# Low halves of the weights made a whole load at a time, over the load itself, and eight load buffers in turn

## The chip, the cores and the metric

One core of one Trainium2 chip runs the kernel. The metric is device time in microseconds for one execution, and a lower number is better. Three runs of the kernel before gave 504.73 to 505.06, median 504.81.

## The reference

The input `x` has 512 rows of 1,024 floats. It is normalised by row, multiplied with `w_in` (1,024 x 6,936) and cut into the inputs of two mixers that work side by side:

```python
h = rms_norm(x, norm_pre)
proj = h @ w_in
(q_n, k_c, v_c, k_s, v_s, k_w, v_w, g_n, z_n,
 q_r, k_r, v_r, z_r, m_a, m_b) = jnp.split(proj, split_points(), axis=-1)
...
y_a = (o_a * jax.nn.silu(z_n)) @ w_nsa_o
...
q_r = apply_rotary(q_r.reshape(B, S, RET_HEADS, RET_QK_DIM), ret_ang)
k_r = apply_rotary(k_r.reshape(B, S, RET_HEADS, RET_QK_DIM), ret_ang) * (RET_QK_DIM ** -0.5)
o_b = jax.vmap(retention_sequence)(q_r, k_r, v_r.reshape(B, S, RET_HEADS, RET_V_DIM))
y_b = (o_b * jax.nn.silu(z_r)) @ w_ret_o
merged = jax.nn.sigmoid(m_a) * y_a + jax.nn.sigmoid(m_b) * y_b
x = x + rms_norm(merged @ w_out, norm_post)
```

`o_a` is sparse attention with a compressed, a selected and a sliding branch (8 heads of 64, two key groups; the compressed keys and values come from a small network with the weights `cmp_w1`, 2,048 x 256, and `cmp_w2`). `o_b` is retention in chunks of 128 rows (4 heads). `apply_rotary` turns pairs of columns that lie half a head apart; the retention heads have 128 columns, all of them turned.

## The kernel before

**Splitting.** A float32 weight is used as the sum of two fp32r numbers, a high half (the rounded weight) and a low half (what rounding left), and so is the other operand. Each product is made of three matmuls: high by high, high by low, low by high (`mm3`). TensorE's work is these matmuls and the transposes (line 263).

**The stream.** All weights lie in one array in the order of use, cut into loads of 128 partitions by 1,024 columns (512 KB; four loads have 560). SyncE's queue issues them (`load_next`, lines 427 and 430) into four buffers `raw`. A load is two *pieces* of 512 columns. For each piece `splitter` has ScalarE (sometimes VectorE, `cp_any`) copy the piece to `whi` (lines 224 and 232), and `split_lo` has VectorE subtract, `wlo = raw - whi` (line 236). `whi` and `wlo` are rings of `NW` = 9 tiles of 512 columns. A piece holds its two tiles until the last matmul that reads it (`used_up`); a buffer `raw` is loaded again as soon as the low halves of both its pieces are made. Some loads (tables of sums for Strassen-like products, the 280-column block, the last four loads) are split into places of their own instead of the ring.

**Stages.** `main` runs them in order: the first block (8 pieces, each used for all four row tiles before the next), a 280-column block, the queries (8 pieces, used once for each of the four row tiles), `hidden` (16 pieces for `cmp_w1`, each used once by four matmuls of 256 columns, while attention's scores, transposes and products stand between them), then the blocks of `PLAN` (gates, retention's inputs, output projections) and `out_seven`. An ordinary block's piece is read in four passes, one for each row tile. Retention's rotation is `tail_qk`: four products of 256 columns with the row's scale and a table (line 249), then a subtraction and an addition. `vals` writes the attention's values as high and low halves, two copies and two subtractions of 64 columns.

**Order.** The program is recorded by a planner (`Order`): coroutines give the time at which they could go on, by a cost for each instruction; the planner takes the first by priority that is due within a margin of its own (`MARGINS`, by coroutine). The order on each engine's queue is fixed by that. `SOON`, `PSOON`, `SLACK` and the hold times belong to the same rules. `load_next` is recorded when a buffer is planned to be free, so the loads stand in SyncE's queue among its other transfers (rotation tables, line 1100, and the signed rows of `x` for the sums, line 606). GpSimd's queue adds up weight sums in DRAM meanwhile (lines 395 and 397).

## Time and profile before

| what | value |
|---|---|
| median of three runs | 504.81 us |
| profiled execution | 504.99 us |
| its span, first to last instruction | 503.2 us |
| TensorE busy | 493.7 us (98%) |
| VectorE busy | 424.6 us (84%) |
| ScalarE busy | 324.7 us (65%) |
| granted TensorE clock, mean | 0.998 |
| instructions | 7,872 |

A busy span of TensorE is not TensorE at its peak, since matmuls overlap: what a matmul costs is read from the distance between the starts of two neighbours. In the same way two VectorE instructions of one kind in a row take less than twice one of them. The chain of waits follows the execution back from its end, and each wait names the last releaser.

### The profile page before, as it was taken

Reading aid. Unit: us, or ns where it says so; the run is one execution under the profiler, and the core shown is the slowest. Engines: PE = TensorE matmul, PEld = TensorE weight load, DVE = VectorE, ACT = ScalarE, POOL = GpSimd, SP = SyncE. Lnnn points to the kernel's source line nnn. Section 1 sums busy time; section 2 is a strip of 40 time slices with the busy share of each in tenths; the row PEclk is TensorE's granted clock in tenths of the full one; section 3 lists DMA queues with packets and bytes.
Section 4 is the critical chain, followed back from the end, with each engine's and each line's share of the span. In section 5 each row is a group of like instructions: output and inputs, shape, how many; then the busy total and the mean of one; then the engine's idle time right before and its main releaser. Section 6 shows DMA issues by size and latency. Waiting matters only on the chain.

```text
span 503.2 us, 7872 instructions
## 1 busy us (share of the span) xinstructions
PE 493.7 (98%) x2666; PEld 421.4 (84%) x2666; DVE 424.6 (84%) x996; ACT 324.7 (65%) x722; POOL 39.3 (8%) x66
## 2 busy tenths in 40 slices
PE   8999999999999999999999999999999999999994
PEld 7898887888888888888888888888888989988883
DVE  6698899989989989998789999778787867979795
ACT  6795599558679788784587574835435535527642
POOL 3102100023000210000100000101000000000010
PEclk9999999999999999999999999999999999999999
DMA  8968995779998899325556673530473735635813
GB/s 318 385 211 283 326 227 200 242 136 225 370 238 182 262 293 211 113 85 166 119 173 212 215 235 114 126 126 8 162 250 113 233 116 191 199 113 169 303 56 142
DMA packets 31080, 98.75 MB, mean 196 GB/s; under 512 B 3136, under 2 KB 6976, under 8 KB 30272
## 3 DMA queue, kind: packets, MB, share of 16 engines
q1 hardware_dynamic: 24576, 70.85, 41.5%
q0 software_dynamic: 6320, 27.26, 22.9%
q8 instruction: 21, 0.34, 0.3%
q14 instruction: 19, 0.16, 0.1%
q10 hardware_dynamic: 144, 0.14, 0.1%
HBM read 93.52 MB, written 31.98 MB: 249 GB/s over the span
## 4 chain that ended last, share of the span: by engine, by line
PE 89%; DMA 5%; DVE 4%; issue 1%; ACT 0%; POOLq 0%; DVEq 0%; POOL 0%; ACTq 0%; SPq 0%
PE bank L257 70%; PE bank L1234 8%; PE bank L1725 7%; PE bank L263 4%; DMA raw<-in_stream_dram 3%; DVE arena_r L236 1%; DMA words<-in_xT_dram 1%; DVE wlo L236 1%; DMA words<-in_x_dram 1%; DVE words L236 1%; DVE words L679 0%; DVE words L249 0%; DVE words L243 0%; DVE words L967 0%; DVE whi L232 0%
## 5 line engine op out<-in xcount | busy, mean ns | idle before, releaser
L224 ACT ACTIVATE whi<-raw 128x512 fp32r<-128x512 f32 x177 | 107.0, 627 | 53.4 <-PE bank L257 36.2
L236 DVE TENSOR_TENSOR wlo<-raw,whi 128x512 fp32r<-128x512 f32 x188 | 123.4, 685 | 10.4 <-ACT whi L224 9.5
L257 PE MATMUL bank<-whi,hTh 128*128 128x512 f32 x192 | 74.0, 407 | 0.3 <-ACT hTh L224 0.3
L257 PE MATMUL bank<-arena_r 128*128 128x256 f32 (+2 forms) x328 | 70.7, 335 | 0.7 <-DVE arena_r L236 0.5
L257 PE MATMUL bank<-whi,hTl 128*128 128x512 f32 x192 | 71.2, 391 | 0.0
L257 PE MATMUL bank<-wlo,hTh 128*128 128x512 f32 x192 | 71.0, 390 | 0.0
L224 ACT ACTIVATE arena_r<-bank 128x512 fp32r<-128x512 f32 (+3 forms) x104 | 49.1, 476 | 26.3 <-PE bank L263 25.4
L236 DVE TENSOR_TENSOR arena_r<-bank,arena_r 128x512 fp32r<-128x512 f32 (+3 forms) x104 | 56.0, 542 | 9.6 <-ACT arena_r L224 8.5
L257 PE MATMUL bank<-arena_r,whi 128*128 128x512 f32 (+1 forms) x208 | 63.6, 381 | 0.0
L224 ACT ACTIVATE words<-words,stat 128x128 f32<-128x128 f32 (+3 forms) x105 | 54.1, 546 | 6.6 <-DVE stat L967 4.9
L257 PEld LDWEIGHTS bank<-arena_r 128*128 128x128 f32 x328 | 50.8, 189 | 7.6 <-DVE arena_r L236 1.2
L257 PE MATMUL bank<-hTh,whi 128*128 128x512 f32 (+1 forms) x144 | 52.2, 363 | 0.0
L257 PE MATMUL bank<-hTh,wlo 128*128 128x512 f32 (+1 forms) x144 | 51.4, 357 | 0.0
L257 PE MATMUL bank<-hTl,whi 128*128 128x512 f32 (+1 forms) x144 | 51.1, 355 | 0.0
L257 PEld LDWEIGHTS bank<-arena_r,whi 128*128 128x128 f32 x208 | 38.8, 188 | 7.3
L257 PEld LDWEIGHTS bank<-whi,hTl 128*128 128x128 f32 x192 | 36.2, 188 | 8.0
L257 PEld LDWEIGHTS bank<-whi,hTh 128*128 128x128 f32 x192 | 36.5, 191 | 6.9 <-ACT hTh L224 0.6
L257 PEld LDWEIGHTS bank<-wlo,hTh 128*128 128x128 f32 x192 | 36.1, 188 | 6.3
L257 PE MATMUL bank<-arena_r,wlo 128*128 128x512 f32 x96 | 37.3, 389 | 0.0
L263 PEld LDWEIGHTS bank<-identr,shorts 128*128 128x128 f32 x268 | 30.1, 140 | 8.6 <-DVE arena_r L236 0.9
L224 ACT ACTIVATE words<-words 128x512 f32<-128x512 f32 (+3 forms) x47 | 27.2, 586 | 12.8 <-DVE words L236 8.0
L263 PE MATMUL bank<-identr,shorts 128*128 128x128 f32 x268 | 31.6, 238 | 0.5 <-DVE arena_r L236 0.5
(182 smaller groups left out, 891.0 us busy)
## 6 DMA issues: line engine op xcount, KB each, us to landing
raw<-in_stream_dram SPq DMA_DIRECT2D x73, 512.0 KB, 4.4
pair<-in_stream_dram POOLq DMA_DIRECT2D x6, 1024.0 KB, 11.8
t<-in_stream_dram POOLq DMA_DIRECT2D x6, 1024.0 KB, 17.2
out<-in_stream_dram POOLq DMA_DIRECT2D x6, 1024.0 KB, 17.1
words<-in_x_dram SPq DMA_DIRECT2D x8, 512.0 KB, 6.9
raw<-s SPq DMA_DIRECT2D x8, 512.0 KB, 4.2
raw<-pair SPq DMA_DIRECT2D x8, 512.0 KB, 4.2
raw<-t SPq DMA_DIRECT2D x8, 512.0 KB, 3.6
```

Of the source, the lines that this page charges most:

```text
L224: S.activation(o, i, func, **kw)
L236: (V if e == "dve" else G).tensor_tensor(o, a, b, op=op)
L257: T.matmul(ps, a, b, start=start, stop=stop)
L263: T.transpose(ps, a, idn)
L1234: T.matmul(ps[m], a, b, start=n in first and s + j == 0, stop=n in last and s + j == 5, skip_group_check=True)
L1725: T.matmul(ps[m], a, b, start=n in first and s + i == 0, stop=n in last and s + i == 5, skip_group_check=True)
```

## The change

The low half of a whole load is made in one subtraction of 1,024 columns and written over the load: each of `NR` = 8 buffers has two names, `raw` (float32) and `rest` (fp32r), at the same address. The tiles `wlo` are gone; `whi` is a ring of five tiles of 1,024 columns (`NW` = 10 pieces), still copied 512 columns at a time. A buffer whose low half lies in it is vacant only when both its pieces are used up; a load that is split into a place of its own frees its buffer after the split. The buffers are taken in the order in which they become vacant. Retention's query and key columns are permuted in the stream, so that the two columns of a rotated pair are neighbours, and `tail_qk` makes two products of 512 columns in place of four of 256. `vals` makes one copy and one subtraction of 2 x 64 columns. One small addition in `ret` goes from VectorE to GpSimd. The planner's table and a score of priorities are other numbers.

```diff
-NR, NW = 4, 9
+NR, NW = 8, 10
...
-MARGIN = 50.0
+MARGIN = 600.0
...
-SOON = 2
-PSOON = 4
+SOON = 4
+PSOON = 3
...
-    nc.alloc_sbuf_tensor("room", [P, 58 * 256], FT)
-    low, made = nc.sbuf_base - 58 * 1024, {}
+    nc.alloc_sbuf_tensor("room", [P, 58 * 256 + NR * 1024 + 128], FT)
+    low, made = nc.sbuf_base - 58 * 1024 - NR * 4096 - 512, {}
+    rawt = [[nc.alloc_sbuf_tensor_at(f"{n}{i}", [P, 1024], dt, offset=low + 58 * 1024 + 320 + i * 4096)
+             for n, dt in (("raw", FT), ("rest", FR))] for i in range(NR)]
...
+    vacant, room = [(0.0, i) for i in range(NR)], []
+
+    def own(i):
+        return KD <= 2 * i < 2 * KD or i in sload or i >= len(loads) - 4
+
+    def may_load():
+        return len(raws) < len(loads) and bool(vacant)
...
-            raw = rp.tile([P, 1024], FT, name="raw", tag="raw", bufs=NR)
-            o, c, r = loads[i][0], 0, parts[2 * (i - NR) + 1][2] if i >= NR else 0.0
...
+        r, b = vacant.pop(0)
+        room.append(b)
+        raw = rawt[b][0].ap()
...
         done.append(r)
+        i = len(done) // 2 - 1
+        if len(done) % 2 == 0 and not own(i):
+            vacant.append((r, room[i]))
+        while may_load():
+            load_next()
...
-                    hi = wp.tile([P, 512], FR, name="whi", tag="whi", bufs=NW)
-                    lo = wp.tile([P, 512], FR, name="wlo", tag="wlo", bufs=NW)
...
+                        hi, lo = wp.tile([P, 1024], FR, name="whi", tag="whi", bufs=NW // 2), rawt[room[i]][1].ap()
...
-                od.spawn(split_lo(p, hi, lo, src, vh, vl, e), rank(p))
+                es.append(e)
                 nxt[0] = p + 1
+                if k:
+                    od.spawn(split_lo(i, hi, lo, src, max(es)), rank(2 * i))
...
-            r = sub_split(vl, src, vh, r)
-        yield lambda: len(parts) == p
-        parts.append((hi, lo, r))
-        if p % 2 and len(raws) <= p // 2 + NR:
-            load_next()
+            r = sub_split(lo[:, :n], src, hi[:, :n], r)
+        yield lambda: len(parts) == 2 * i
+        for k in range(2):
+            c = slice(k * n // 2, (k + 1) * n // 2)
+            parts.append((hi[:, c], lo[:, c], r))
+        if own(i):
+            vacant.append((r, room[i]))
+            while may_load():
+                load_next()
...
-        for g in range(2):
-            sv = src[:, g * 64:(g + 1) * 64]
-            e = act(VS[:, t, br, g, g, :], sv, r=r)
-            e = sub_split(VS[:, t, br, g, 1 - g, :], sv, VS[:, t, br, g, g, :], e)
-        return e
+        sv, b = src.rearrange("p (g c) -> p g c", g=2), VS[:, t, br, 0, 0, :]
+        hi, lo = (bass.AP(tensor=b.tensor, offset=b.offset + o, ap=[list(b.ap[0]), [n, 2], [1, 64]]) for o, n in ((0, 192), (64, 64)))
+        return sub_split(lo, sv, hi, act(hi, sv, r=r))
...
-                    od.spawn(att_unit(t, g, brs, slots, stat), 2)
+                    od.spawn(att_unit(t, g, brs, slots, stat), 0)
...
-        for i in range(2):
-            e = stt(v1[:, :, i, :], pv[:, :, i, :], rs(t), tv[:, 0], OP.mult, OP.mult, e)
+        c = [tv[:, i].unsqueeze(2).broadcast_to([P, 256, 2]) for i in range(2)]
+        e = stt(v1, pv, rs(t), c[0], OP.mult, OP.mult, e)
         yield e, "dve"
-        stt(v2[:, :, 0, :], pv[:, :, 1, :], rs(t), tv[:, 1], OP.mult, OP.mult, e)
-        e = stt(v2[:, :, 1, :], pv[:, :, 0, :], rs(t), tv[:, 1], OP.mult, OP.mult, e)
+        e = stt(v2, pv, rs(t), c[1], OP.mult, OP.mult, e)
...
-        ev = ts(rv, mv[:, :, 1], 1e-6, None, OP.add, r=e)
+        G.tensor_scalar(rv, mv[:, :, 1], 1e-6, None, op0=OP.add)
+        ev = od.op("pool", 80.0, e, True)
```

Three places show how the order moved. The first is VectorE's queue at the very start, where `raw_55` (before: `raw`) is the first load and `hTl` the low half of the normalised input's first 128 columns. Before:

```order
L483 CAST whi<-raw 128x512
L249 SCALAR_TENSOR_TENSOR hTl<-words_264_165,hTh 128x256
L249 SCALAR_TENSOR_TENSOR hTl<-words_512_108,words_264_165,hTh 128x256
L243 TENSOR_SCALAR ngp<-words_264_165 128x8
L236 TENSOR_TENSOR wlo<-raw,whi 128x512 x2
```

After:

```order
L498 CAST whi<-raw_55 128x512
L237 TENSOR_TENSOR rest_56<-raw_55,whi 128x1024
L250 SCALAR_TENSOR_TENSOR hTl<-words_264_178,hTh 128x256
L250 SCALAR_TENSOR_TENSOR hTl<-words_512_121,words_264_178,hTh 128x256
L244 TENSOR_SCALAR ngp<-words_264_178 128x8
L233 CAST whi<-raw_57 128x512
```

The weights' low half, which needs both high halves, stands ahead of the input's low half, where it stood behind it.

The second is VectorE's queue in the middle of `hidden`, where `arena_r<-bank` is the low half of transposed attention weights, `stat` a softmax sum and `ISA` the largest score of a row. Before:

```order
L236 TENSOR_TENSOR arena_r<-bank_88,arena_r 128x512
L232 CAST whi<-raw 128x512
L236 TENSOR_TENSOR wlo<-raw,whi 128x512 x3
L236 TENSOR_TENSOR arena_r<-bank_89,arena_r 128x512
L253 RECIPROCAL stat_857<-stat_857 128x4
L236 TENSOR_TENSOR stat_857<-stat_857,gate 128x4
L236 TENSOR_TENSOR wlo<-raw,whi 128x512
L236 TENSOR_TENSOR arena_r<-bank_88,arena_r 128x512
```

After:

```order
L233 CAST whi<-raw_61 128x512
L233 CAST whi<-raw_55 128x512
L237 TENSOR_TENSOR rest_62<-raw_61,whi 128x1024
L237 TENSOR_TENSOR rest_56<-raw_55,whi 128x1024
L237 TENSOR_TENSOR words_128_709<-words_512_141,cst 128x128
L237 TENSOR_TENSOR words_128_710<-words_512_141,cst 128x8x8 x2
L237 TENSOR_TENSOR words_512_141<-words_128_709,words_128_710 128x8x16
L254 RECIPROCAL stat_814<-stat_814 128x4
L237 TENSOR_TENSOR stat_814<-stat_814,gate 128x4
L237 TENSOR_TENSOR arena_r<-bank_101,arena_r 128x512
L237 TENSOR_TENSOR arena_r<-bank_102,arena_r 128x512
L237 TENSOR_TENSOR rest_58<-raw_57,whi 128x1024
```

Low halves of `hidden` now stand ahead of the attention's work instead of among it, and a cast of the load `raw_55`, the first of `hidden`'s second half, stands ahead of the low halves `rest_62` and `rest_56`.

The third is SyncE's queue after the signed rows, from the load that follows the first rotation table. Before, by the numbers of the buffers' uses:

```order
L606 DMA s0_148<-words14336_512_115 128x256
L606 DMA s2_150<-words14336_512_115 128x256
L1100 DMA words28672_512_136<-in_rope_r_dram 128x512
L427 DMA raw_906<-in_stream_dram 128x1024
L427 DMA raw_954<-in_stream_dram 128x1024
```

After:

```order
L628 DMA s2_163<-words14336_512_128 128x256
L1120 DMA words28672_512_149<-in_rope_r_dram 128x512
L437 DMA raw0_55<-in_stream_dram 128x1024
L437 DMA raw1_57<-in_stream_dram 128x1024
L437 DMA raw4_63<-in_stream_dram 128x1024
L437 DMA raw5_65<-in_stream_dram 128x1024
L437 DMA raw2_59<-in_stream_dram 128x1024
```

All loads of `hidden`'s first half stand ahead of this table in the queue in both kernels. `raw0_55` is its fifth load, the first of its second half; in the changed kernel it waits until TensorE has read the first load of the queries for the last time, where before it waited for low halves to be made.

## The prediction, made before the changed kernel was run

> **What bounds the kernel now.** I read the page first, then busy time by stretches, then TensorE's timeline where a stretch is not full.

> ```profile
> span 503.2 us, 7872 instructions
> PE 493.7 (98%) x2666; PEld 421.4 (84%) x2666; DVE 424.6 (84%) x996; ACT 324.7 (65%) x722; POOL 39.3 (8%) x66
> PE 89%; DMA 5%; DVE 4%; issue 1%; ACT 0%; POOLq 0%; DVEq 0%; POOL 0%; ACTq 0%; SPq 0%
> ```

> The chain of waits is TensorE for 89%. So the floor is TensorE's own work, and only time in which it waits can be won. Its pace where nothing disturbs it (columns: start, length, instruction), and its end:

> ```profile
> 485.63 5.60 PE L1725 MATMUL bank<-arena_r 128*128 128x512 f32 x24
> ...
> 496.29 0.39 PE L1725 MATMUL bank<-arena_r,hTh 128*128 128x512 f32 x1
> ```

> 24 matmuls take 5.60, of which the last one has 0.39 for itself: 5.21 for 23 steps, 0.227 us for 512 columns. After the last one (496.29 + 0.39) come 6.5 us of norm and output.

> Busy time by stretch (length, then PE, PEld, DVE, ACT) shows where TensorE isn't full:

> ```profile
> 71.00:85.00 14.00, 12.58 (x86) 10.47 (x85) 13.58 (x33) 13.91 (x31) 0.00 (x0) 1.00 0.70 221
> ```

> From 71 to 85 us, in `hidden`, VectorE and ScalarE are both over 96% busy and TensorE is not. A piece of `hidden` costs TensorE only four matmuls of 256 columns, the splitting engines as much as any other. The waits there, in TensorE's timeline:

> ```profile
> 73.03 0.45 PE L257 MATMUL bank<-arena_r 128*128 128x512 f32 x1
> 74.02 0.50 PE L257 MATMUL bank<-arena_r 128*128 128x512 f32 x1 [0.54 <-DVE arena_r L236]
> ...
> 75.30 0.28 PE L257 MATMUL bank<-wlo,arena_r 128*128 128x256 f32 x1
> 75.42 0.28 PE L257 MATMUL bank<-whi,arena_r 128*128 128x256 f32 x1
> 76.16 0.38 PE L257 MATMUL bank<-wlo,arena_r 128*128 128x256 f32 x1 [0.47 <-DVE wlo L236]
> ...
> 82.29 0.28 PE L257 MATMUL bank<-wlo,arena_r 128*128 128x256 f32 x1
> 82.87 0.54 PE L263 MATMUL bank<-identr,shorts 128*128 128x128 f32 x4 [0.30 <-DVE arena_r L236]
> ```

> The first step is 0.99 us where 0.23 would do, the second (75.42 to 76.16) 0.74 for the 0.12 of a normal one (75.30 to 75.42), the third 0.58 for 0.12: 0.76 + 0.62 + 0.46 = 1.84 us. Smaller steps of the same kind up to 86 us (for instance 83.94 to 84.33) bring it to about 3.0 by my count of starts, so 1.2 of it is an estimate from many rows.

> **The start: slower by 0.74.** TensorE, VectorE and ScalarE in the first microseconds:

> ```profile
> 4.71 2.02 PE L257 MATMUL bank<-whi,hTh 128*128 128x512 f32 x4 [0.30 <-ACT hTh L224]
> 6.56 1.07 PE L257 MATMUL bank<-whi,hTl 128*128 128x512 f32 x4
> ...
> 4.69 0.48 DVE L249 SCALAR_TENSOR_TENSOR hTl<-words,hTh 128x256 fp32r<-128x256 f32 x1 [0.38 <-ACT hTh L224]
> 5.09 0.48 DVE L249 SCALAR_TENSOR_TENSOR hTl<-words,words,hTh 128x256 fp32r<-128x256 f32 x1
> ...
> 4.96 0.61 ACT L224 ACTIVATE whi<-raw 128x512 fp32r<-128x512 f32 x1
> ```

> Today `hTl` is ready at 5.17, long before TensorE asks for it at 6.56. In the new order the low half of the first load stands ahead of it on VectorE, and that one needs ScalarE's second high half, ready at 4.96 + 0.61 = 5.57. Its length is that of the only subtraction of 1,024 columns in the trace:

> ```profile
> L236 DVE TENSOR_TENSOR arena_r<-words,arena_r 128x1024 fp32r<-128x1024 f32 x2 | 2.4, 1213 | 0.0
> L236 DVE TENSOR_TENSOR wlo<-raw,whi 128x512 fp32r<-128x512 f32 x188 | 123.4, 685 | 10.4 <-ACT whi L224 9.5 <-PE bank L257 0.4
> ```

> 5.62 + 1.21 = 6.83, less 0.07 of overlap and plus 0.48 gives 7.24, and 0.06 later TensorE goes on: 7.30 for 6.56. The second half of `hTl`, 0.40 later, is in time for the third matmul (7.30 + 0.45). Bounds: 0.4 if the subtraction starts earlier, 1.1 if its full length is kept. Later low halves of the first block are ready a microsecond or more ahead, and so hide.

> **`hidden`: faster by 1.8.** Prices on VectorE are distances between starts; the first row is TensorE's first score in the old order:

> ```profile
> 59.87 0.63 PE L257 MATMUL bank<-arena_r 128*128 128x512 f32 x2
> ...
> 58.56 0.55 DVE L236 TENSOR_TENSOR words<-words,cst 128x128 f32<-128x128 f32 x3
> ...
> 60.53 0.69 DVE L967 CUSTOM_DVE_ANT_0 words<-bank,maskp 128x512 f32<-128x512 f32 x1 [0.97 <-PE bank L257]
> ...
> 62.09 1.39 DVE L236 TENSOR_TENSOR arena_r<-bank,arena_r 64x512 fp32r<-64x512 f32 x2
> ...
> 65.55 0.69 DVE L236 TENSOR_TENSOR wlo<-raw,whi 128x512 fp32r<-128x512 f32 x1
> 66.16 0.68 DVE L967 CUSTOM_DVE_ANT_0 words<-bank,maskp 128x512 f32<-128x512 f32 x1
> 66.77 0.08 DVE L967 DVE_READ_ACCUMULATOR2_ANT stat<- 128x1 f32 x1
> ...
> 73.89 0.42 DVE L232 CAST whi<-raw 128x512 fp32r<-128x512 f32 x1
> 74.22 1.89 DVE L236 TENSOR_TENSOR wlo<-raw,whi 128x512 fp32r<-128x512 f32 x3
> ...
> 84.19 1.89 DVE L236 TENSOR_TENSOR wlo<-raw,whi 128x512 fp32r<-128x512 f32 x3
> ```

> Three low halves of 512 take 1.89 (twice): 0.60 each plus 0.085 of overlap. One of 1,024 then takes 1.213 - 0.085 = 1.13, against 1.20 for two: only 0.07 saved for each load. The order counts for more: in the changed queue fewer attention pieces stand between the eight loads. From the first score reduction to the low half of `hidden`'s last load stand 8 reductions (66.16 to 66.77: 0.62), 7 low halves (1.13), 2 query rotations (0.55 and an addition: 0.8), 4 attention low halves (as `wlo`, 0.60), 4 casts (73.89 to 74.22: 0.33), one pair of 64 x 512 (1.3) and 1.4 of small work (an estimate): 20.9 us. TensorE's matmuls from the first score to the end of `hidden` add up to 21.9 at their paces (0.227 for 512 columns, 0.12 for 256, 0.073 for a transpose, from the rows on transposes below). VectorE begins 0.65 later (60.53 to 59.87), and the last load needs 0.85 after its low half: 0.65 + 20.9 + 0.85 = 22.4, so at least 0.5 of waiting is left; pieces that are late in the middle add to that, and I take 1.2 for the 3.0 of today. Bounds: 0 left and 3.0 left.

> [...]

> **A wait at 33 us: 0.3 gained.**

> ```profile
> 33.26 0.29 PE L257 MATMUL bank<-arena_r,hTl 128*128 128x280 f32 x1
> 33.71 0.37 PE L263 MATMUL bank<-identr,shorts 128*128 128x128 f32 x2 [0.16 <-DVE arena_r L236]
> ```

> 0.45 for a step of 0.13. TensorE comes there 0.74 later and VectorE has less to do (wider low halves, one `vals` pair for two), so it goes; bounds 0 and 0.33.

> **Transposes: 0.5 gained.** A matmul behind transposes starts late:

> ```profile
> 60.33 0.45 PE L263 MATMUL bank<-identr,shorts 128*128 128x128 f32 x4
> 60.62 0.70 PE L257 MATMUL bank<-arena_r 128*128 128x512 f32 x2
> 61.16 0.39 PE L257 MATMUL bank<-whi,hTh 128*128 128x512 f32 x1
> ```

> 0.54 for two instead of 0.45: 0.08 each time that TensorE leaves transposes. The built order has 69 such groups where it had 75: 6 x 0.08. The number of matmuls and transposes is the same.

> **Costed at nothing.** *Buffers.* Of eight, up to five hold low halves, so three or four loads are under way, as with the four before. In steady state a load of an ordinary block is read in four passes over 20 us, and the next four loads come meanwhile; a load takes

> ```profile
> raw<-in_stream_dram SPq DMA_DIRECT2D x73, 512.0 KB, 4.4
> ```

> 4.4 us. Without that cover it costs what the late load makes TensorE wait (first rival). The rotation tables behind the loads in SyncE's queue have the same cover. *Rotations, `vals`, the addition on GpSimd.* Four products of 474 ns become two near 746:

> ```profile
> L249 DVE SCALAR_TENSOR_TENSOR words<-bank,rs,words 128x256 f32<-128x256 f32 x16 | 6.9, 474 | 0.0
> L249 DVE SCALAR_TENSOR_TENSOR words<-words,rr,words 128x512 f32<-128x512 f32 x6 | 4.1, 746 | 0.0
> ```

> 0.4 less for each of eight tails, if columns with a gap run as fast, which no row shows; the timeline names no wait of TensorE after 95 us, so this cannot be seen, and a loss is covered as well. GpSimd's addition precedes a power that only a later scaling needs. *The end.* The last twelve instructions of VectorE and ScalarE are the same; 6.5 us stay.

> **Sum.** Against the profiled execution: 504.99 + 0.74 - 1.8 - 0.3 - 0.5 = 503.13. The median is 0.18 below that execution, so 502.95, say 503.0. With the bounds of the terms this case reaches from 502.1 to 504.1.

> **Rivals.** *Loads late (slower).* VectorE's queue has the cast of `raw_55` ahead of `rest_62` and `rest_56`. That load is now issued when TensorE has left the first query load, ten matmuls (2.3 us, and 0.2 as an estimate for SyncE) after the first score. The cast is reached 0.65 + 10.3 = 11.0 us after that score (8 reductions, 2 low halves, a rotation, the 64 x 512 pair, a cast and 0.7 of small work stand ahead of it): 8.5 us of room. For: the weight sums move beside it, and such transfers were slow in the chain of waits and on the page:

> ```profile
> 9.66 7.84 DMA raw<-in_stream_dram
> ...
> pair<-in_stream_dram POOLq DMA_DIRECT2D x6, 1024.0 KB, 11.8
> ```

> Against: 4.4 is the median. Above 8.5 us everything behind the cast moves, and TensorE with it; at 11.8 the loss is 3.3: 506.3. It makes the change slower from 11.3 us on.

> *The order buys nothing.* If other pieces are late in their turn, 3.0 stays in `hidden` and 0.3 at 33 us: 504.81 + 0.74 - 0.5 = 505.0. For: ScalarE was fuller than VectorE there (13.91 of 14 us), and its copies stay 512 wide.

> *All waits go.* No wait left in `hidden`: 503.0 - 1.2 = 501.8. For: the arithmetic leaves only 0.5.

> *The clock.* TensorE runs its first matmuls at half pace (four in 1.85 us from 4.71) and is at full pace from 6.56. The new wait falls just there. If it had to earn its pace again, and for as long as it took from the span's start, 6.56 us at half pace lose 3.3: 506.3. [...]

> **How the numbers follow.** Forecast 0.47, nothing bought 0.19, all waits gone 0.16, loads late 0.14, clock 0.04. A measurement of this kernel can tell about 0.2% (1.0 us) from no change, so faster is below 503.8 and slower above 505.8. Of the forecast 0.38 lies below 503.8 and 0.09 above; faster is 0.38 + 0.16 = 0.54. The same is 0.09 with nearly all of "nothing bought": 0.27. Slower is 0.14 + 0.04 with a rest of 0.01: 0.19. The range 501.5 to 506.3 takes in the forecast, both near rivals with their bounds and part of the late loads.

> **What would show it.** Right: TensorE's first `hTl` matmul near 7.3; steps over 0.3 us between 71 and 86 us adding to about 1.2; no wait near 33 us; TensorE's last matmul near 494.8; the end 6.5 us long. Wrong: `hTl` in time; a wait for `raw` ahead of VectorE's casts; waits of TensorE after 95 us, of which none is left today; a first block still at half pace after 7.3.

## The result and the profile after

The changed kernel takes 507.94 us (median of six runs, 507.19 to 509.23), the kernel before 504.92 in the same rounds. The ratio is 1.0064 with a 95% interval of 1.0049 to 1.0078: 3 us slower. The forecast was 503.0, the range 501.5 to 506.3, so both missed, and the sign with them. The profiled execution took 507.20 us at a granted clock of 0.998; its span grew from 503.2 to 505.4. Three of the six runs had spans of 506.8 to 507.4 and a clock of 0.992 to 0.993. So of the 3.0 us, 2.2 lie between the two profiled executions, both at 0.998, and the rest of the median comes from these three runs.

From the page of the changed kernel: span, busy time, the wide low half among the groups of instructions, and the loads among the transfers (KB each, median us to landing):

```profile
span 505.4 us, 7750 instructions
PE 493.3 (98%) x2666; PEld 420.4 (83%) x2666; DVE 420.1 (83%) x880; ACT 309.9 (61%) x688; POOL 43.8 (9%) x74
...
L237 DVE TENSOR_TENSOR rest<-raw,whi 128x1024 fp32r<-128x1024 f32 x94 | 113.6, 1220 | 11.5 <-ACT whi L225 11.0
...
raw<-in_stream_dram SPq DMA_DIRECT2D x73, 512.0 KB, 5.1
```

The engines have less to do (VectorE 4.5 us less, ScalarE 14.8), the wide low half costs 1,220 ns as forecast, and yet the span is 2.2 us longer. So the loss is time in which TensorE waits.

**Where it went.** I count TensorE's *loss*: for each matmul or transpose, the distance to the start of the next one, less the pace of its form in long undisturbed rows (0.2267 us for 512 columns, 0.1133 for 256, 0.127 for 280, 0.058 for 128; the rare ones of 384 and 64 columns count 0.17 and 0.06). Summed by stretch of the profiled executions, in us; `before_again`, `after_again` and the rest are runs of the experiments below:

| stretch, us | before | after | before_again | after_again | e2_rsrow | e4_row | e8_cast | e5_narrow |
|---|---|---|---|---|---|---|---|---|
| 0 to 20 | 3.80 | 4.63 | 5.20 | 6.64 | 7.58 | 4.82 | 4.96 | 7.18 |
| 20 to 40 | 1.07 | 0.79 | 0.49 | 0.58 | 0.55 | 1.45 | 0.90 | 0.56 |
| 40 to 60 | 1.22 | 3.06 | 1.36 | 3.02 | 1.21 | 1.23 | 1.22 | 2.91 |
| 60 to 100 | 5.90 | 4.54 | 5.57 | 4.44 | 4.64 | 4.51 | 4.73 | 6.19 |
| 100 to 220 | 8.11 | 7.86 | 8.19 | 7.88 | 7.66 | 7.87 | 7.80 | 8.20 |
| 220 to 240 | 1.00 | 2.20 | 1.02 | 2.30 | 2.30 | 1.39 | 1.36 | 2.67 |
| 240 to the end | 4.96 | 5.15 | 5.01 | 5.21 | 5.21 | 5.13 | 5.09 | 6.97 |
| sum | 26.06 | 28.23 | 26.84 | 30.07 | 29.15 | 26.40 | 26.06 | 34.68 |

From before to after the sum grows by 2.17, the span by 2.2: the count holds all of it. Three stretches lose most (0.83, 1.84 and 1.20), and two gain most (0.28 and 1.36).

**The start.** TensorE's and VectorE's timeline of the changed kernel (start, length, instruction, idle time before it):

```profile
4.60 1.55 PE L258 MATMUL bank<-whi,hTh 128*128 128x512 f32 x4 [0.20 <-ACT hTh L225]
7.24 1.19 PE L258 MATMUL bank<-whi,hTl 128*128 128x512 f32 x4 [1.09 <-DVE hTl L250]
...
5.57 1.23 DVE L237 TENSOR_TENSOR rest<-raw,whi 128x1024 fp32r<-128x1024 f32 x1 [1.29 <-ACT whi L225]
6.71 0.48 DVE L250 SCALAR_TENSOR_TENSOR hTl<-words,hTh 128x256 fp32r<-128x256 f32 x1
```

The wide low half begins at 5.57 and the first `hTl` matmul at 7.24 (forecast: 7.30). TensorE stood still for 1.09 us.

**`hidden`.** The stretch of before in the changed kernel (busy time of each engine, clock, DMA share):

```profile
71.00:85.00 14.00, 13.20 (x91) 11.43 (x90) 13.28 (x29) 13.97 (x30) 0.00 (x0) 1.00 1.03 376
```

The two waits that its timeline still names between 70 and 87 us:

```profile
79.34 0.50 PE L258 MATMUL bank<-arena_r 128*128 128x512 f32 x1 [0.36 <-DVE arena_r L237]
83.65 0.39 PE L258 MATMUL bank<-rest,arena_r 128*128 128x256 f32 x1 [0.44 <-DVE rest L237]
```

TensorE is busy for 13.20 of 14 us instead of 12.58; ScalarE is still full.

**A new wait at 53 us.** TensorE, ScalarE and VectorE of the changed kernel:

```profile
52.95 0.40 PE L258 MATMUL bank<-whi,hTl 128*128 128x512 f32 x1
54.98 0.36 PE L264 MATMUL bank<-identr,shorts 128*128 128x128 f32 x2 [1.63 <-ACT rsrow L225]
...
52.44 2.00 ACT L225 ACTIVATE arena_r<-words 128x1024 fp32r<-128x1024 f32 x2 [3.50 <-DVE words L237]
54.35 0.58 ACT L225 ACTIVATE rsrow<-bank 128x512 f32<-128x512 f32 x1
...
51.54 1.75 DVE L237 TENSOR_TENSOR words<-bank,cst 64x256 f32<-64x256 f32 x4 [0.29 <-PE bank L264]
```

TensorE's next transposes need a bank that the row of scales still lies in (`norms`; line 656 of the changed kernel copies it to `rsrow`). That copy stands behind two copies of 1,024 columns (`x_split`, line 801 there), and these wait 3.50 us for VectorE. In the kernel before, the same copy stood four rows ahead of them:

```profile
46.47 0.60 ACT L224 ACTIVATE rsrow<-bank 128x512 f32<-128x512 f32 x1 [2.47 <-PE bank L263]
...
52.37 2.30 ACT L224 ACTIVATE arena_r<-words 128x1024 fp32r<-128x1024 f32 x4 [0.34 <-DVE words L236]
```

**New waits after 220 us.** TensorE and VectorE of the changed kernel:

```profile
233.41 0.39 PE L258 MATMUL bank<-whi,hTl 128*128 128x512 f32 x1
234.37 0.50 PE L258 MATMUL bank<-whi,hTh 128*128 128x512 f32 x1 [0.57 <-DVE words L250]
...
230.36 0.75 DVE L250 SCALAR_TENSOR_TENSOR words<-bank,rs,words 128x512 f32<-128x512 f32 x1
231.12 0.69 DVE L237 TENSOR_TENSOR words<-words,words 64x512 f32<-64x512 f32 x1
231.83 1.23 DVE L237 TENSOR_TENSOR rest<-raw,whi 128x1024 fp32r<-128x1024 f32 x1
232.97 0.68 DVE L237 TENSOR_TENSOR arena_r<-bank,arena_r 128x512 fp32r<-128x512 f32 x1
233.57 0.74 DVE L250 SCALAR_TENSOR_TENSOR words<-bank,rs,words 128x512 f32<-128x512 f32 x1
```

The accumulator stays taken until the rotation's second product at 233.57 has read it, and three other pieces stand between that and the first. A strided product of 512 columns takes 0.74 to 0.75 us, the price that the forecast had as an estimate: its length is not the trouble, its place is.

### The profile page after: what moved, and what is told of

Read it like the earlier page. It is cut to its first block, busy times and chain, and to the rows that moved or that the text cites. A ratio compares the mean times of both kernels' runs of the same rounds, so it can differ in the third digit from the quotient of the medians.

```text
span 505.4 us, 7750 instructions
## 1 busy us (share of the span) xinstructions
PE 493.3 (98%) x2666; PEld 420.4 (83%) x2666; DVE 420.1 (83%) x880; ACT 309.9 (61%) x688; POOL 43.8 (9%) x74
## 4 chain that ended last, share of the span: by engine, by line
PE 90%; ACT 4%; DVE 2%; issue 2%; DMA 1%; POOLq 0%; POOL 0%; DVEq 0%; ACTq 0%
PE bank L258 72%; PE bank L1253 8%; PE bank L1745 7%; PE bank L264 4%; ACT words L225 2%; ACT arena_r L225 1%; ACT whi L225 1%; DVE rest L237 1%; DMA words<-in_x_dram 1%; DVE words L250 1%; DVE words L237 1%; DVE arena_r L237 0%; ACT hTh L225 0%; ACT rsrow L225 0%; POOLq L2003 0%
## 5 line engine op out<-in xcount | busy, mean ns | idle before, releaser
L225 ACT ACTIVATE whi<-raw 128x512 fp32r<-128x512 f32 x161 | 94.5, 627 | 71.4 <-PE bank L258 44.9
L237 DVE TENSOR_TENSOR rest<-raw,whi 128x1024 fp32r<-128x1024 f32 x94 | 113.6, 1220 | 11.5 <-ACT whi L225 11.0
L258 PE MATMUL bank<-rest,hTh 128*128 128x512 f32 x192 | 71.1, 390 | 0.0
L225 ACT ACTIVATE words<-words,stat 128x128 f32<-128x128 f32 (+3 forms) x100 | 52.6, 551 | 6.4 <-DVE stat L237 4.3
L258 PE MATMUL bank<-hTh,rest 128*128 128x512 f32 (+1 forms) x144 | 51.1, 355 | 0.0
L258 PEld LDWEIGHTS bank<-rest,hTh 128*128 128x128 f32 x192 | 36.2, 188 | 6.2
L258 PE MATMUL bank<-arena_r,rest 128*128 128x512 f32 x96 | 37.3, 389 | 0.0
L237 DVE TENSOR_TENSOR words<-bank,words 128x512 f32<-128x512 f32 (+3 forms) x48 | 28.1, 592 | 6.1 <-PE bank L258 2.2
## 6 DMA issues: line engine op xcount, KB each, us to landing
raw<-in_stream_dram SPq DMA_DIRECT2D x73, 512.0 KB, 5.1
pair<-in_stream_dram POOLq DMA_DIRECT2D x6, 1024.0 KB, 11.3
t<-in_stream_dram POOLq DMA_DIRECT2D x6, 1024.0 KB, 17.2
out<-in_stream_dram POOLq DMA_DIRECT2D x6, 1024.0 KB, 15.7
words<-in_x_dram SPq DMA_DIRECT2D x8, 512.0 KB, 7.1
raw<-s SPq DMA_DIRECT2D x8, 512.0 KB, 4.6
raw<-pair SPq DMA_DIRECT2D x8, 512.0 KB, 5.2
raw<-t SPq DMA_DIRECT2D x8, 512.0 KB, 3.7
```

The source lines that it names most:

```text
L225: S.activation(o, i, func, **kw)
L237: (V if e == "dve" else G).tensor_tensor(o, a, b, op=op)
L258: T.matmul(ps, a, b, start=start, stop=stop)
```

## The experiments

The order on all engines hangs on the planner's arithmetic, so that an edit of it moves pieces everywhere. The moves below therefore leave the planner's account as it is and change only where an instruction is written into its queue. They are read in two ways: by the ratio to the kernel before in the same rounds, and by the loss in the stretch that the move touches.

**e1_start.** The first low half behind the input's:

```diff
-            r = sub_split(lo[:, :n], src, hi[:, :n], r)
+            if i == 0:
+                held.append((lo, src, f(hi)))
+                r = od.op("dve", 1.042 * n + 69, r, True)
+            else:
+                r = sub_split(lo[:, :n], src, hi[:, :n], r)
...
+        if k == 0:
+            lo, src, hi = held.pop()
+            for c in (slice(0, 512), slice(512, 1024)):
+                V.tensor_tensor(lo[:, c], src[:, c], hi[:, c], op=OP.subtract)
         od.flags.add(f"h{k}")
```

> The changed kernel, with one thing moved: the first load's low half stands behind the input's two low halves on VectorE, in two pieces of 512 columns, as it did before the change. Theory (the gap at the start costs its own 0.8 us and also makes the longer runs, those of 508.6 to 509.2 at a granted clock of 0.992): the first hTl matmul starts near 6.5, and all runs lie within 0.3 of 506.4. Rival 1 (the gap costs only itself): two groups stay, near 506.4 and near 508. Rival 2 (the start lies under a later wait): 507.2 and 508.6 to 509.2 as now.

Measured: 508.45, ratio 1.0053 (1.0037 to 1.0069), runs from 506.91 to 509.90. The first gap is gone, but none of the three statements fits the runs: in the profiled one (509.9) the next part of the input and the second load landed late (ScalarE waits for the one until 7.94, VectorE for the other until 10.00), and TensorE waited twice in the next steps. Its timeline:

```profile
8.72 1.20 PE L258 MATMUL bank<-whi,hTh 128*128 128x512 f32 x4 [0.97 <-ACT hTh L225]
11.15 1.73 PE L258 MATMUL bank<-whi,hTl 128*128 128x512 f32 x4 [1.23 <-DVE hTl L250]
```

Its stretches (the column after POOL's is the granted clock):

```profile
11.00:12.00 1.00, 0.85 (x3) 0.70 (x4) 1.00 (x3) 1.00 (x2) 0.00 (x0) 0.80 1.07 422
12.00:13.00 1.00, 1.00 (x4) 0.81 (x3) 1.00 (x2) 0.43 (x2) 0.00 (x0) 0.50 1.03 416
...
14.00:15.00 1.00, 1.00 (x4) 0.81 (x3) 1.00 (x2) 0.73 (x2) 0.00 (x0) 0.50 1.08 422
15.00:16.00 1.00, 1.00 (x6) 0.83 (x5) 1.00 (x2) 0.65 (x1) 0.00 (x0) 0.99 1.01 395
```

The clock falls to half at 11.60 (0.80 is 0.40 of a microsecond at half) and comes back at 15.02: 3.42 us at half pace, worth half of that, 1.7. The start differs this much from run to run, so the verdict on it had to come from other runs.

**e2_rsrow.** ScalarE's copy of the row of scales ahead of `x_split`'s:

```diff
+        row.append(ps)
         yield e, "act"
-        rwr[0] = act(rsrow, ps, r=e)
+        first()
+        rwr[0] = od.op("act", act_ns(rsrow, ps), e)
...
+    def first():
+        while row:
+            S.activation(rsrow, row.pop(), AF.Copy)
...
+        first()
         e = act(xs[:, :, 0, :], v)
```

> The changed kernel, with one thing moved: ScalarE's copy of the row of scales (rsrow) stands ahead of the two copies of 1,024 columns of x_split. Theory (the copy holds the bank that TensorE's transposes wait for at 53 us, and nothing else is late there): the wait of 1.63 us goes, and the time falls by 1.8: 505.4 in the short runs, 506.8 to 507.4 in the long ones, with the start as it is. Rival (another piece of ScalarE's or VectorE's queue, which are both held up by the 64-row tails, is late next): a wait of over 1 us stays between 52 and 58 us, and the time falls by less than 0.8: 506.4 or more.

Measured: ratio 1.0036 (1.0020 to 1.0052), shortest runs 505.16 and 505.34. ScalarE and TensorE of this run, which is 2.9 us later because of its start:

```profile
54.86 0.60 ACT L666 ACTIVATE rsrow<-bank 128x512 f32<-128x512 f32 x1 [3.09 <-PE bank L264]
55.35 2.00 ACT L225 ACTIVATE arena_r<-words 128x1024 fp32r<-128x1024 f32 x2
...
55.81 0.40 PE L258 MATMUL bank<-whi,hTl 128*128 128x512 f32 x1
56.05 0.28 PE L264 MATMUL bank<-identr,shorts 128*128 128x128 f32 x2
```

The transposes no longer wait, the loss from 40 to 60 us falls from 3.06 to 1.21, what the kernel before has there (1.22), and no stretch behind it gets worse by more than 0.1. The theory holds for this wait: 1.84 of the 2.2 us is the place of one copy. The longer runs reach 509.95, where it gave at most 507.4, so the times above the shortest have another cause. This run also shows the other way in which the start costs time:

```profile
5.14 2.08 PE L258 MATMUL bank<-whi,hTh 128*128 128x512 f32 x4 [0.74 <-ACT hTh L225]
7.73 2.08 PE L258 MATMUL bank<-whi,hTl 128*128 128x512 f32 x4 [0.52 <-DVE hTl L250]
9.61 1.91 PE L258 MATMUL bank<-rest,hTh 128*128 128x512 f32 x4
11.31 1.87 PE L258 MATMUL bank<-whi,hTh 128*128 128x512 f32 x4
13.02 1.09 PE L258 MATMUL bank<-whi,hTl 128*128 128x512 f32 x4
```

Four matmuls take 1.07 to 1.09 at full pace; here half pace lasts to 13.0, where the profiled run of before had it to 6.56. The clock column says 1.00 all the while (in every row from 4 to 14 us of this run): it shows a fall from full pace, 0.50 in `e1_start`, not a full pace that has not come yet.

**e6_fill, b1_gap, b2_gapfill.** Whether idleness costs more than itself. `e6_fill` keeps TensorE at work in the gap of the changed kernel, `b1_gap` makes such a gap in the kernel before, `b2_gapfill` fills that one:

```diff
                         yield hready[k] + PE_LAG
+                        for _ in range(0 if k else 3):
+                            T.matmul(banks[0][:, 0:P], rsrow[:, 0:P], rsrow[:, 0:P], start=True, stop=True)
```

```diff
                     V.tensor_copy(vh, src)
+                    for _ in range(5):
+                        V.tensor_tensor(rsrow[:, 128:384], x0[:, KD:KD + 256], x0[:, KD:KD + 256], op=OP.add)
```

> The changed kernel, with three more matmuls of 128 x 128 on zeros (nothing reads their result) between the first four hTh matmuls and the first hTl one, so that TensorE is not idle for the whole 1.1 us there. Theory (idleness in the first 8 us is what makes the longer runs): the gap's own 0.8 stays, and all runs lie within 0.3 of 507.2 at a clock of 0.996 or more. Rival (the longer runs have another cause): some of the runs lie at 508.6 to 509.2 still.

> The kernel before, with five additions of 128 x 256 (results not used) on VectorE behind its first cast, so that the input's low halves come 1.6 us later and TensorE waits about 0.7 us ahead of its first hTl matmul, as in the changed kernel. Theory (the gap costs itself and makes the longer runs): short runs near 505.6, and some runs 1.4 to 2.0 above these at a clock near 0.992. Rival (the gap costs only itself): all runs near 505.6. Second rival (the loss at the start is given back at later waits): near 504.9.

> b1_gap with three more matmuls of 128 x 128 on zeros in the gap that it makes (results not used). Theory (TensorE's idleness in the gap makes the long runs at a clock of 0.994): no run of over 506.5, where b1_gap had 3 of 11. Rival (what is late is made by something else): some runs at 506.8 to 507.4 at a clock of 0.994 still.

Measured: `e6_fill` 507.23 to 508.16, none at a clock below 0.997; two of its five runs lie above the 507.5 of its theory, and its profile still has 0.78 us of idleness in the gap. `b1_gap` 1.0008 (0.9997 to 1.0019), of 11 runs three at 506.78 to 507.41 and a clock of 0.994. `b2_gapfill` 1.0006 (0.9996 to 1.0016), none of 12 below 0.996; four still took 506.58 to 507.04, against the letter of the theory, and the one of them with a profile (507.04) had half pace up to 10.2 us, so full pace came late there and did not fall. In `b1_gap`'s profile the gap itself (0.63 in the first 20 us) is given back at once: the loss from 20 to 40 us falls from 1.07 to 0.54, since the wait at 33 us goes when TensorE comes later. So the gap's own price is mostly returned there, and its further price is the clock. The 0.63 is itself a net figure, since full pace came at 5.16 in this run and at 6.53 in that of before.

**e4_row, e7_wake.** Both moves above, and the second product of the third and fourth rotation behind the first; `e7_wake` has `WAKE = 8` besides:

```diff
+ROW = ((0, 2), (0, 3))
...
         e = stt(v1, pv, rs(t), c[0], OP.mult, OP.mult, e)
+        if (hp, t) in ROW:
+            V.scalar_tensor_tensor(v2, pv, rs(t), c[1], op0=OP.mult, op1=OP.mult)
         yield e, "dve"
-        e = stt(v2, pv, rs(t), c[1], OP.mult, OP.mult, e)
+        if (hp, t) in ROW:
+            e = od.op("dve", 1.042 * 512 + 130, e)
+        else:
+            e = stt(v2, pv, rs(t), c[1], OP.mult, OP.mult, e)
```

> The changed kernel with three moves: the first load's low half behind the input's low halves, in two pieces; ScalarE's copy of rsrow ahead of x_split's copies; and, for the third and fourth query and key tails, the second product of the rotation right behind the first on VectorE. Theory (after the start, the change loses 1.84 at 53 us and 1.2 between 220 and 240 us and gains the rest): against the changed kernel TensorE's loss falls by about 1.8 in the stretch from 40 to 60 us and by about 1.2 from 220 to 240, and the time is 1.0 to 1.7 below that of the kernel before in the same rounds (ratio 0.9966 to 0.998). Rival (the low halves or the transposes that now stand behind the moved instructions are late instead): under half of either loss goes, and the ratio is 1.000 or more.

> The three moves of e4_row, and eight warm-up matmuls instead of seven, so that TensorE is busy to 4.9 us and not to 4.4, up to the first real matmul. Theory (TensorE's pace is granted after a stretch of about 3.4 us of nearly unbroken work, in stretches whose beginning differs from run to run, so that idleness before 8 us costs up to a further stretch at half pace): the median is 0.3 to 1.0 below that of e4_row, and the runs lie closer together. Rival (the pace at the start doesn't hang on idleness): the same median as e4_row, or 0.2 more, since the first real matmul waits for the warm-up.

Measured: `e4_row` 505.16 against 505.18, ratio 0.9994 (0.9985 to 1.0002). VectorE has the products at

```profile
228.92 0.75 DVE L251 SCALAR_TENSOR_TENSOR words<-bank,rs,words 128x512 f32<-128x512 f32 x1
229.59 0.74 DVE L1154 SCALAR_TENSOR_TENSOR words<-bank,rs,words 128x512 f32<-128x512 f32 x1
```

and TensorE's wait for the bank is gone; 0.8 of the 1.2 comes back (2.20 to 1.39), the rest is a wait for a low half at 224 us that stayed. With three moves the 3 us are gone, but the 1.0 to 1.7 below the kernel before are not reached. `e7_wake`: 504.79, ratio 0.9993 (0.9984 to 1.0003); the median is 0.37 lower than `e4_row`'s, which the intervals don't tell from nothing. The stretches of its theory show in the traces, 3.413 us long (the moments at which the clock changed are below).

**e5_narrow.** Each low half but the first as two instructions in the same place:

```diff
-            r = sub_split(lo[:, :n], src, hi[:, :n], r)
+            for c in (slice(0, n // 2), slice(n // 2, n)) if i else (slice(0, n),):
+                V.tensor_tensor(lo[:, c], src[:, c], f(hi[:, c]), op=OP.subtract)
+            r = od.op("dve", 1.042 * n + 69, r, True)
```

> The changed kernel, with each low half made as two instructions of half the columns, except the first, in the same place of VectorE's order. Theory of the prediction (a wide low half hides its fixed time and so takes the waits of the hidden layer from 3.0 to what they are): TensorE's loss from 60 to 100 us rises from 4.5 to about 5.9, what the kernel before loses there. Rival (the new order took those waits): it stays within 0.3 of 4.5.

Measured, one run: 513.64. The loss from 60 to 100 us rises from 4.54 to 6.19, and the waits there are now

```profile
82.55 0.51 PE L258 MATMUL bank<-arena_r 128*128 128x512 f32 x1 [0.83 <-DVE arena_r L237]
98.03 0.36 PE L264 MATMUL bank<-identr,shorts 128*128 128x128 f32 x2 [1.00 <-DVE arena_r L237]
```

So the gain in `hidden` needs the width: without it 1.65 us come back, more than the 1.36 that the change had won there. The 186 low halves of 512 columns take 689 ns each in this run, one of 1,024 took 1,220 in the changed kernel: 158 ns less than two of them, the fixed time of the theory. The prediction had given most of this gain to the order and 0.07 us for each load to the width. Half pace to 12.1 us adds to this run, and 1.8 more is lost after 240 us.

**after_again, s1_cast, e8_cast.** The changed kernel once more on another chip; and the cast of half of the second load, which now stands ahead of the input's second low half on VectorE, behind it (alone, and with e4's moves):

```diff
+                elif p in (2, 3) and od.begin("act", r) + act_ns(h, v) > od.begin("dve", r, True) + copy_ns(h, v) + DVE_BIAS:
+                    casts.append((h, v))
+                    e = od.op("dve", copy_ns(h, v), r, True)
...
+        while k == 1 and casts:
+            V.tensor_copy(*casts.pop())
         od.flags.add(f"h{k}")
```

> The changed kernel itself, word for word, beside the next three on one chip. Expected from the earlier runs: a ratio of 1.004 to 1.008 to the kernel before, runs in more than one group. Where the second load lands after 8.4 us, TensorE waits a second time in the first 12 us (theory), or it does not (rival: that wait belongs to the moved pieces of e1_start and e4_row alone).

> The changed kernel, with one thing moved: VectorE's cast of half of the second load stands behind the input's second low half instead of ahead of it. Theory (the change has put the second hTl behind a load; before, it waited for no load): the second row of hTl matmuls does not wait any more, worth 0 where the load lands by 8.4 us, and 0.5 to 1.1 us where it lands at 9 to 10; the median is 0.2 to 1.0 below that of after_again. Rival (that wait comes in the moved kernels alone): the same median.

> The three moves of e4_row, and the cast behind the input's second low half as in s1_cast. Theory (start, row of scales, second product and cast are all that the change loses): the second row of hTl matmuls waits for nothing, and the time is 0.8 to 1.7 below that of the kernel before (ratio 0.9966 to 0.9984). Rival (what comes first in those 12 us is the input itself, whichever order VectorE has): the same as e4_row, a ratio of 0.999 to 1.0005.

Measured: `after_again` 1.0062 (1.0045 to 1.0080), `s1_cast` 1.0062 (1.0039 to 1.0084): no effect of the cast shows, and the theory on it falls. In `after_again` the second load landed at 8.68, and TensorE did not wait a second time in the first 12 us, so that theory falls too. `e8_cast` 505.04, 0.9995 (0.9985 to 1.0005), as `e4_row`. But two profiles caught what the longer runs are. The stretches of `after_again` behind its gap, in which TensorE was idle from 6.20 to 7.63:

```profile
7.00:8.00 1.00, 0.37 (x2) 0.30 (x2) 1.00 (x4) 1.00 (x2) 0.00 (x0) 1.00 0.95 377
8.00:9.00 1.00, 1.00 (x4) 0.81 (x3) 0.34 (x2) 0.41 (x2) 0.00 (x0) 0.61 1.09 418
9.00:10.00 1.00, 1.00 (x4) 0.78 (x3) 1.00 (x3) 0.96 (x2) 0.00 (x0) 0.50 1.01 414
...
11.00:12.00 1.00, 1.00 (x4) 0.76 (x4) 1.00 (x3) 0.63 (x1) 0.00 (x0) 0.68 1.10 432
```

and those of `s1_cast` behind the wait at 53 us:

```profile
56.00:57.00 1.00, 1.00 (x6) 0.86 (x5) 0.31 (x1) 0.58 (x2) 0.00 (x0) 0.71 0.99 315
57.00:58.00 1.00, 1.00 (x3) 0.76 (x3) 0.85 (x4) 0.50 (x1) 0.00 (x0) 0.50 1.02 303
...
59.00:60.00 1.00, 1.00 (x5) 0.84 (x4) 1.00 (x2) 0.80 (x2) 0.00 (x0) 0.58 1.04 319
```

Half pace from 8.22 to 11.64 and from 56.42 to 59.84, 3.42 us both times; in `s1_cast` the loss from 40 to 60 us is 4.47 instead of 3.06, so the fall costs 1.4 on top of the wait.

**t1_code.** The changed code with the table of margins, `SOON`, `PSOON`, `SLACK` and the hold times of the kernel before (the table, for short).

> The changed code (wide low halves, eight buffers, interleaved rotation, its numbers of priority at each step) with the table of margins of the kernel before. Theory (the code brings the gain in the hidden layer, the table brings the two waits at 53 and at 220 to 234 us): TensorE's loss stays below 4.9 between 60 and 100 us, is below 1.5 between 40 and 60 and below 1.3 between 220 and 240, and the time is at or below that of the kernel before. Rival (any other table moves pieces somewhere, and code and table can't be told apart): losses of over 1.5 us in other stretches, and a time of more than 506.

Measured: 515.63, ratio 1.0203 (1.0185 to 1.0222), with losses of 2.7 to 4.4 us in five stretches of 20 us. In time the rival holds: code and table work only together. From 60 to 100 us 8.25 is lost, so wide low halves alone do not bring the gain in `hidden`. But two statements of the theory come true: the loss is 1.43 from 40 to 60 us and 0.48 from 220 to 240, since with the old table the copy stands ahead of `x_split`'s and the two products stand together:

```profile
48.50 0.60 ACT L225 ACTIVATE rsrow<-bank 128x512 f32<-128x512 f32 x1 [2.32 <-PE bank L264]
...
53.87 2.01 ACT L225 ACTIVATE arena_r<-words 128x1024 fp32r<-128x1024 f32 x2
...
230.19 1.40 DVE L250 SCALAR_TENSOR_TENSOR words<-bank,rs,words 128x512 f32<-128x512 f32 x2
```

So the new code does not bring the two new waits by itself; they need the new table.

**s2_wait, s2_fill.** `e8_cast` with the copy of `rsrow` back behind `x_split`'s, without and with work for TensorE in the wait that returns:

```diff
+        if idle and idle[0] is ps:
+            idle.pop()
+            for _ in range(6):
+                T.matmul(banks[7][:, 0:P], ident, ident, start=True, stop=True)
         for g in range(2):
             e = tr(ps[:, g * P:(g + 1) * P], kd[:, off + g * P:off + (g + 1) * P], ident, r)
```

> e8_cast with the copy of rsrow back behind x_split's copies, as in the changed kernel: so the wait at 53 us comes back, and nothing else. Theory (a wait of 1.6 us there costs 1.8 by itself, and in part of the runs TensorE also falls to half pace behind it): the shortest runs lie 1.8 above the shortest of e8_cast (near 505.9), and about a third of the runs 1.4 above these, at a clock near 0.993. Rival (the clock falls at the start alone): all runs 1.8 above e8_cast's, at a clock of 0.996 to 0.998.

> s2_wait with six matmuls of 128 x 128 on the identity (results not used) in a free bank, just ahead of the transposes that wait at 53 us, so that TensorE works through most of the wait. Theory (idleness makes the fall): the runs lie 1.8 to 2.1 above e8_cast's, and none has a clock below 0.995. Rival (the fall has another cause): the same groups as s2_wait.

Measured: `s2_wait` 1.0049 (1.0030 to 1.0069), five runs at 506.31 to 507.51 and three at 508.80 to 510.29 with a clock of 0.993 to 0.994; the loss from 40 to 60 us is 2.96 again, where `e8_cast` has 1.22. `s2_fill` 1.0022 (1.0011 to 1.0032), nine runs at 505.75 to 507.21, all clocks 0.996 or more. In `s2_fill`'s timeline the six matmuls, twelve entries there, take 1.50 us, most of the wait, and the transposes come as late as they did (its profile has another wait, of 1.48 us, at 30 us, with no fall behind it):

```profile
53.45 1.50 PE L730 MATMUL bank<-ident 128*128 128x128 f32 x12
55.25 0.37 PE L265 MATMUL bank<-identr,shorts 128*128 128x128 f32 x2 [0.30 <-ACT rsrow L226]
```

**e9_wake, before_again.** `e8_cast` with `WAKE = 8`, and the kernel before for its profile.

> e8_cast with eight warm-up matmuls instead of seven. Theory (the first stretch of work is unbroken to the first real matmul, so full pace comes one stretch earlier in the runs that get it late): the median is 0.2 to 0.8 below the kernel before (ratio 0.9984 to 0.9996) and no run has a clock below 0.995. Rival (the warm-up is long enough as it is): a ratio of 0.9995 as e8_cast.

> The kernel before, word for word, for its profile on the chip of this call. Theory (the loads at the start land later on this chip than on the first one, so that TensorE loses more than 3.8 us in the first 20 us also here, and the moved kernels' 4.8 to 5.0 there are no loss to it): 4.5 or more. Rival (the order at the start of the changed kernel still loses about 1 us): near 3.8.

Measured: `e9_wake` 504.94 against 505.41, 0.9993 (0.9984 to 1.0002), no clock below 0.996. `before_again` 0.9999, and its start

```profile
4.94 2.08 PE L257 MATMUL bank<-whi,hTh 128*128 128x512 f32 x4 [0.54 <-ACT hTh L224]
6.81 1.91 PE L257 MATMUL bank<-whi,hTl 128*128 128x512 f32 x4
8.52 1.42 PE L257 MATMUL bank<-wlo,hTh 128*128 128x512 f32 x4
```

has half pace to 9.2 us and a loss of 5.20. That is over 4.5, as the theory said, but late loads are not the main reason: TensorE's first matmul comes only 0.23 us later than in the first profile of before (4.94 for 4.71), and half pace behind it lasts 4.3 us instead of 1.8, which costs 1.2. `e8_cast` has 3.8 us at half pace there, and its loss behind that matmul is half of this, 1.91, so in its profile the start costs nothing but the late pace. Against this profile `e8_cast` loses 0.78 less (0.84 of it in `hidden`, 0.39 from 100 to 220 us, 0.34 more from 220 to 240), by its runs 0.3. No version beats the kernel before by more than the measurement can tell.

**Idleness and the clock in all runs.** Runs with a granted clock of 0.994 or less:

| kernels | such runs |
|---|---|
| kernel before, in the rounds of the experiments | 0 of 98 |
| gap at the start or wait at 53 us, or both (after, after_again, s1_cast, e1_start, e2_rsrow, b1_gap, s2_wait) | 19 of 55 |
| the same with TensorE at work in one of them (e6_fill, b2_gapfill, s2_fill) | 0 of 26 |
| neither (e4_row, e7_wake, e8_cast, e9_wake) | 1 of 45 |

All four runs of `t1_code` had 0.994 or less as well; it waits in many places, up to 2.38 us at once. The bound of 0.994 misses some falls: the profiled run of `e1_start` has one at a mean clock of 0.995. The mean also takes in the end, where the clock halves after TensorE's last matmul (`before`: 0.50 from 501.46 us on, the last matmul's end is at 496.67), so means of 0.996 to 0.999 do not differ by a fall. Long runs at such a mean (`after_again`, 509.43 and 509.95 at 0.996) must have another cause; full pace that comes late, as in `e2_rsrow`, would be one, but no profile of these two runs shows it.

**Why the same wait costs some runs a fall.** Each trace keeps the moments at which the clock changed. In all 18 traces they lie whole multiples of 3.413 us apart: in `s1_cast` at 5.22, 56.42, 59.84 and, behind the end, 503.57, which are 15, 1 and 130 such steps; in the profile of before at 6.53 and 501.46 (145 steps), in that of the changed kernel at 5.40 and 503.75 (146). Where the steps begin differs from run to run. So each run divides into stretches of its own, and TensorE's idle time can be added up in each, from the first full pace to the half pace behind the last matmul (the ends of matmuls in a profile are modelled, so hundredths are not sure). With 1.49 us or less no stretch was followed by a fall, with 2.12 or more each of 19 was (18 at the end of a run, one in `t1_code`). Between them lie nine stretches of 1.62 to 1.77, and three were followed by a fall: `e1_start` (1.76), `s1_cast` (1.63) and `after_again` (1.62). Three of the other six hold the wait at 53 us whole, 1.63 each (after, `e6_fill`, `e1_start`). Where a border divided the wait at 53 us (1.15 and 0.47 in `s2_wait`, 0.75 and 0.87 in `after_again`), no fall came either. So the wait at 53 us, 1.63 us of idleness, is at the edge of what brings a fall, and whether one stretch holds all of it is chance.

## Why the prediction was wrong

- **The start, 0.74:** right as to place and size in the first profile (7.24 for 7.30; the loss grew by 0.83). What it missed is that later waits can give most of it back (0.53 of 0.63 in `b1_gap`).
- **The wait at 33 us, 0.3:** it went, by 0.28. But it goes in `b1_gap` and in `before_again` (0.49 for 1.07) as well, where nothing changed but TensorE's lateness. So the term came true by TensorE's lateness, which the prediction named, and the work taken from VectorE need have no part in it.
- **`hidden`, 1.8:** right in direction and place, too large in size: 1.36 in the first pair of profiles, 0.84 to 1.13 in the second. Steps more than 0.2 us over their pace between 71 and 86 us add to 2.37 before and to 1.13 after, for the 3.0 and 1.2 of the prediction; so the mis-sized part is the estimate of 1.2 from small steps, 0.5 by this count. Its division between order and width was wrong: neither brings the gain alone (`e5_narrow`, `t1_code`).
- **Transposes, 0.5:** the traces have 69 groups of them for 75, the six fewer of the prediction. From 100 to 220 us 0.25 to 0.39 less is lost; that it is these groups was not shown.
- **Costed at nothing, and the step that failed:** "the timeline names no wait of TensorE after 95 us, so this cannot be seen, and a loss is covered as well". That timeline was the old order's. In the new order the second product gives its bank back 0.73 us after TensorE wants it (234.37 for 233.64). And ScalarE's queue between the start and 71 us was in no term; there its copy of `rsrow` moved behind two copies that wait for VectorE. The two stretches cost 3.0 us, and moving three instructions took 2.6 of it back (`e4_row`).
- **The range of the sum:** the lowest bounds of all its terms together give 501.4 and the highest 505.4; the 502.1 to 504.1 that it states is narrower than its own bounds. The measured 507.94 lies outside either.
- **The rival "the clock", 0.04:** right in kind, with a price of 3.3 where a fall costs 1.4 to 1.7, and a chance that was far too small. The chance was the author's estimate; the trace of before has the clock fall only behind TensorE's last matmul, at 501.46. The price took the half pace to last as long as from the span's start, 6.56 us; the three falls named here lasted 3.42 each (`e1_start`, `after_again`, `s1_cast`). TensorE was not idle for all of that time before a fall: 1.43 us of idleness in one piece, 1.62 in the stretch, was enough in `after_again`. And the steps of 3.413 us begin at another place in each run, with full pace at 6.53 in the profile of before and at 5.40 in that of the changed kernel, and the prediction didn't use it.
- **The other rivals:** "loads late" did not come: a load takes 5.1 us instead of 4.4, ScalarE and VectorE wait for some, but TensorE's timeline names no wait behind one after the start. "The order buys nothing" and "all waits go" failed from 60 to 100 us, by the loss there.

So the cause is shown for 1.84 us at 53 (`e2_rsrow`, `s2_wait`) and for 0.8 from 220 to 240 (`e4_row`), and for the fall of the clock behind either wait (19 of 55 runs, 0 of 26 when filled, the kernels taken together). Open are the wait of 0.36 at 224 us, the one low run of `e8_cast`, and what decides between 1.62 and 1.77 us of idleness in a stretch: a fall followed the wait at 53 us in `s1_cast`, and not in the changed kernel, `e6_fill` or `e1_start`.

## What to carry to other kernels

When a change brings a new order, the trace of before covers nothing: walk the new order along each engine for every bank that TensorE needs back, and ask what now stands ahead of the instruction that frees it, on ScalarE as well as on VectorE. A cheap instruction that releases a bank belongs ahead of long ones that wait for something else: here a copy of 0.58 us behind two that take 2.00 and waited 3.50 for VectorE cost 1.84. Where TensorE's idleness in one stretch of 3.413 us added up to 1.62 to 1.77, the clock fell behind three of nine; with matmuls of no use in a gap, 0 of 26 runs had a granted clock of 0.994 or less, where 19 of 55 had it without them. And a start with little idleness was worth more than its own microseconds: with 0.30 full pace came at 6.56 us (before), with 0.74 and 0.52 at 13.0 (`e2_rsrow`).
